# Gate products of a gated recurrence: eight matmuls a tile over stacked high and low parts, in place of twelve

## The chip, the cores and the metric

One core of a Trainium2 chip runs the program. The metric is device time in microseconds, and less is better. Before the change it was 1309.05 us, the median of three runs from 1308.57 to 1309.22.

## What is computed

A hybrid encoder of two layers takes one step for two groups of tokens that share the weights: 512 prompt tokens and 32 sample tokens, 544 columns in all. Each layer multiplies the stream by `w_in`, and the columns of the result feed three branches: attention in a band of chunks (A), retention (B) and a gated recurrence (C). The branches are gated and merged, and a projection, a per-layer embedding and a LayerNorm follow. The change is in branch C, of which the reference says:

```python
xpad = jnp.concatenate([s_conv.astype(xr.dtype), xr], axis=1)
xc = conv_b + sum(xpad[:, j:j + t] * conv_w[j] for j in range(CONV_W))
...
xb = xc.reshape(b, t, N_BLOCKS_C, BLOCK_C)          # 8 blocks of 64 channels
r = sigmoid(einsum('btni,nij->btnj', xb, w_gate_a) + b_gate_a)
ig = sigmoid(einsum('btni,nij->btnj', xb, w_gate_x) + b_gate_x)
log_a = -LRU_C * r * softplus(-lru_lambda)
a = jnp.exp(log_a)
bx = jnp.sqrt(-jnp.expm1(2.0 * log_a)) * ig * xc
h = scan of  h = a * h + bx
```

So each of eight blocks of 64 channels is multiplied by two 64 x 64 matrices, one for each gate.

## The kernel before

Activations lie transposed in SBUF: a tile has 128 channels on the partitions and the tokens along the free dimension. Every weight matrix is cut into blocks of 128 x 128, which come from HBM in chunks of eight (512 KB, `raw`). Every number that goes into a large product is split into a high part in a format that TensorE multiplies fast (fp32r) and a low part, the rest. `hilo` (lines 263 to 265) does that for activations: ScalarE casts the high part, VectorE subtracts it from the source. `split` (lines 208 to 213) does the same for weights, half a chunk at a time. A product is then three: high by high, high weight by low activation, low weight by high activation. One weight block over 544 tokens is therefore six matmuls (three products in two column spans), issued by `block` at line 256, and the text calls these six a block.

The order of the whole program is written out by a small planner in Python; the hardware queues then run it in that order, each engine for itself. `UNITS` lists the products of a layer: `xr` tiles 0 and 1 as a pair (16 blocks), `xr` 2, `xr` 3, then `va` 0 to 3, `qa` and `ka` in turn, and so on, 8 blocks each. Before each block the loop calls `tick` (line 174). A tick first lets `stream` (line 219) split weights up to eight blocks ahead, and then resumes those side jobs whose time has come:

```python
def add(job, delay=1):
    jobs.append([job, clock[0] + delay])
...
    stream(LEAD if clock[0] > 8 else 2)
    for j in list(jobs):
        while j[1] <= clock[0]:
            d = next(j[0], None)
```

Side jobs are generators; the numbers that they yield are steps of this clock, one step a block, and stand in the table `PACE`. When the second half of a chunk is split, `load` (line 195) issues the transfer of a later chunk into the buffer that was read last: this transfer waits in SP's queue for the subtraction that reads the buffer. All transfers of the program are issued by SP, in program order.

The recurrence is such a side job. When an `xr` tile is finished, `evac` copies it into `xrp` (lines 899 and 900) and adds `lru_tile(t)` (line 904). This computes the convolution `xc`, 547 columns (512 prompt tokens, three columns of padding and state, 32 sample tokens), with one instruction on ScalarE and three on VectorE; waits `lt1` = 8 steps; splits it with `hilo`; waits `lt2` = 5 steps; and then for each of the two gates issues six matmuls (line 522) with block-diagonal weights of 128 x 128 that hold two 64 x 64 matrices, over two halves of 274 columns in two PSUM banks, followed by three sigmoids on ScalarE (lines 525 to 527). The gates are `lt3` = 3 steps apart. At the end GpSimd multiplies the second gate by `xc` (lines 529 and 530). Four tiles make a layer; tile 1 begins 8 steps after the pair is done, and the others 2 steps after their product. After tile 3 the job `lru_job` does Exp, Tanh, Sqrt and the scan. In the same stretch the `va` tiles come out of TensorE, are copied from PSUM (line 866), and turned by TensorE later (`va_job`). Attention begins when the turned v, the gates and the first K are there (line 367).

PSUM has four kinds of buffers: `mm` (two of two banks each, for the large products), `sc` (two banks), `tp` (one) and `pv` (one). Small tiles in SBUF come from the pool `tmp` with 14 buffers.

Of the kernel before, what the change touches and what calls it, by code (L numbers as in the profile page):

```python
# [9 lines left out]
F32 = mybir.dt.float32  # L10
F32R = mybir.dt.float32r
AF = mybir.ActivationFunctionType
ALU = mybir.AluOpType
MUL, ADD, SUB = ALU.mult, ALU.add, ALU.subtract
# [3 lines left out]
NP, NS = 512, 32  # L18
N = NP + NS
# [36 lines left out]
def blocks_of(kind):  # L56
# [5 lines left out]
NB = len(BLOCKS)  # L62
NCH = NB // 8
AT = {k: BLOCKS.index((k, 0, 0)) for k in ("xr", "wg", "pg")}
# [5 lines left out]
PACE = {  # L70
# [5 lines left out]

# [10 lines left out]

P_CW, P_CB, P_BA, P_BX, P_LAM, P_GN, P_LG, P_LB = 0, 16, 20, 24, 28, 32, 36, 44
P_SC, P_SL = 52, 64
P_S0 = 68  # L90
NPAR = P_S0 + 256


# [30 lines left out]
def encoder(ctx: ExitStack, tc, xT, pT, W, RB, KC, VC, PAR, CST, LGB, o_y, o_k, o_v, o_rp, o_rs, o_cv, o_lr):  # L124
    nc = tc.nc
    V, S, G, T, Q = nc.vector, nc.scalar, nc.gpsimd, nc.tensor, nc.sync
# [6 lines left out]
    tp_ = pool("tmp", 14)  # L133
# [9 lines left out]
    def sl(name, dt=F32, shape=(128, 4, N)):  # L143
        return slab.tile(list(shape), dt, tag="slab", name=name)

    def tmp(name, shape=(128, N)):
        return tp_.tile(list(shape), F32, tag="tmp", name=name)

    def psum(kind):
        if kind == "mm":  # L150
            return ps_mm.tile([128, 1024], F32, tag="mm", name="mm")
        return {"sc": ps_sc, "tp": ps_tp, "pv": ps_pv}[kind].tile([128, 512], F32, tag=kind, name=kind)
# [18 lines left out]
    def add(job, delay=1):  # L171
        jobs.append([job, clock[0] + delay])
# [19 lines left out]
    raw, parts, held = {}, {}, {}  # L192
# [70 lines left out]
    def hilo(h, lo, src):  # L263
        S.copy(h, src)  # L264
        V.tensor_tensor(lo, src, h.bitcast(F32), SUB)  # L265
# [59 lines left out]
    def layer(l, env, nxt):  # L325
        pa = par[l]

        def pcol(c, t):
            return pa[:, c + t:c + t + 1]
# [172 lines left out]
        W547 = NP + 3 + NS  # L502

        def lru_tile(t):
            if t == 0:
                env["lru"] = [sl("lru_r"), sl("lru_i"), sl("lru_a")]
            R, I, _ = env["lru"]
            xrp = env["xrp"]
            xc = tmp("xc", (128, W547))
            S.activation(xc, xrp[:, t, 0:W547], AF.Identity, scale=pcol(P_CW, t), bias=pcol(P_CB, t))  # L510
            for j in range(1, 4):
                V.scalar_tensor_tensor(xc, xrp[:, t, j:j + W547], pcol(P_CW + 4 * j, t), xc, MUL, ADD)
            yield PACE["lt1"]
            xch, xcl = (tp_.tile([128, W547], F32R, tag="tmp", name="xch") for _ in range(2))
            hilo(xch, xcl, xc)
            yield PACE["lt2"]
            for g in range(2):
                w, lo = ([parts[(l * NB + AT["wg"] + g * 4 + t) // 4][i][:, t] for i in range(2)])
                ps = psum("sc"), psum("pv")
                for i, (wg, x) in enumerate(((w, xch), (w, xcl), (lo, xch))):  # L520
                    for p_, c0 in ((ps[0], 0), (ps[1], W547 - 274)):
                        T.matmul(p_[:, :274], lhsT=wg, rhs=x[:, c0:c0 + 274], start=i == 0, stop=i == 2)  # L522
                d = (I if g else R)[:, t]
                b_ = pcol(P_BX if g else P_BA, t)
                S.activation(d[:, :274], ps[0][:, :274], AF.Sigmoid, bias=b_)
                S.activation(d[:, 274:NP], ps[1][:, 1:NP - 273], AF.Sigmoid, bias=b_)
                S.activation(d[:, NP:], ps[1][:, 274 - NS:274], AF.Sigmoid, bias=b_)
                yield PACE["lt3"]
            G.tensor_tensor(I[:, t, :NP], I[:, t, :NP], xc[:, :NP], MUL)
            G.tensor_tensor(I[:, t, NP:], I[:, t, NP:], xc[:, NP + 3:], MUL)  # L530
            if t == 3:
                env["gates"] = True
                add(lru_job())

        def lru_job():
            R, I, A = env["lru"]

            for t in range(4):
                S.activation(A[:, t], R[:, t], AF.Exp, scale=sp[:, 1, l, t:t + 1])
                S.activation(R[:, t], R[:, t], AF.Tanh, scale=sp[:, 0, l, t:t + 1])  # L540
                yield PACE["lru0"]
            y = I
            for t in range(4):
                r, a = R[:, t], A[:, t]
                V.scalar_tensor_tensor(r, a, 1.0, r, ADD, MUL)
                V.tensor_scalar(a, r, -1.0, 1.0, MUL, ADD)
                V.scalar_tensor_tensor(r, a, 1.0, r, ADD, MUL)
                yield PACE["lru1"]
            for t in range(4):
                S.activation(R[:, t], R[:, t], AF.Sqrt)  # L550
                yield PACE["lru2"]
            for t in range(4):
                G.tensor_tensor(R[:, t], R[:, t], I[:, t], MUL)
                yield PACE["lru3"]
                V.tensor_tensor_scan(y[:, t, :NP], A[:, t, :NP], R[:, t, :NP], 0.0, MUL, ADD)
                V.tensor_tensor_scan(y[:, t, NP:], A[:, t, NP:], R[:, t, NP:], pcol(P_SL, t), MUL, ADD)
            yield 2
            env["yc"] = y
            Q.dma_start(out=o_lr[l, :, :, 0:1], in_=y[:, :, NP - 1:NP])
            Q.dma_start(out=o_lr[l, :, :, 1:2], in_=y[:, :, N - 1:N])  # L560
# [20 lines left out]
        def ret_job():  # L581
# [41 lines left out]
            g128 = bc(cst[:, C_G128:C_G128 + 4], [[1, 4], [0, 64]])  # L623
            s0 = e3(pa[:, P_S0:P_S0 + 256])
            for c in range(4):
# [230 lines left out]
        def evac(kind, t, ps, hf=None):  # L856
            pv = ps[:, MM0:MM0 + N]
            if kind in KEY:
# [3 lines left out]
                d = env[key][:, t]  # L862
                if kind == "kb":
                    S.mul(d, pv, 0.125)
                else:
                    S.copy(d, pv)
                if kind == "ka":
                    if t == 0:
                        env["KTh"], env["KTl"] = sl("KTh", F32R), sl("KTl", F32R)
# [23 lines left out]
            elif kind == "xr":  # L893
# [7 lines left out]
                if t == 3:  # L901
                    Q.dma_start(out=o_cv[l, :, :, 0:3], in_=xrp[:, :, NP:NP + 3])
                    Q.dma_start(out=o_cv[l, :, :, 3:6], in_=xrp[:, :, NP + NS + 3:NP + NS + 6])
                add(lru_tile(t), PACE["lt00"] if t == 1 else PACE["lt0"])
            elif kind in ("za", "zb", "zc"):
                for f in {"za": ("ya1", "ya2"), "zb": ("yb",), "zc": ("yc",)}[kind]:
                    need(env, f)
                y = env["y" + kind[1]]
                if t == 0:
                    env[kind] = (sl(kind + "h", F32R), sl(kind + "l", F32R))  # L910
                h, lo = env[kind]
# [12 lines left out]
            elif kind[0] == "b":  # L924
                sg = env.pop(("sg", t))
                a, b = t // 4, t % 4
# [19 lines left out]
            elif kind == "wo":  # L946
                a, b = t // 4, t % 4
                if b == 0:
                    env["r", a] = sl("r")
                r, xh_, xl_ = env["r", a][:, b], st["xh"][a][:, b], st["xl"][a][:, b]  # L950
# [48 lines left out]
        for group in UNITS:  # L999
            kind, t = group[0]  # L1000
# [27 lines left out]
            for k in range(nk):  # L1028
                for ps in pss:
                    a, b = k // 4, k % 4  # L1030
# [117 lines left out]
```

## Time and profile before

| | us |
|---|---|
| median of three runs | 1309.05 |
| the profiled execution's own time | 1308.99 |
| its span, from the first to the last instruction | 1307.2 |
| TensorE busy (matmul) | 1290.2 |
| VectorE busy | 719.6 |
| ScalarE busy | 547.0 |
| GpSimd busy | 176.3 |

The engines are written PE (TensorE), ACT (ScalarE), DVE (VectorE), POOL (GpSimd) and SP, which issues the transfers; SPq is its queue. In a row of the timeline the first number is the start in microseconds from the beginning of the span and the second the duration; then come the engine, the line of the kernel, the operation, the tile that is written and after the arrow those that are read, partitions by elements, and how many such instructions the row merges. What stands in brackets is the idle time before it and what ended that. In a row of transfers the last number is the median time from issue to landing.

### The profile page before, as it was taken

The page shows a single profiled execution, that of the slowest core. Times are in us where ns is not written, and L with a number is a line of the kernel's source. Part 1 is how long each engine was busy: PE and PEld are TensorE (multiplying, and loading weights), DVE is VectorE, ACT ScalarE, POOL GpSimd, SP SyncE. Part 2 cuts the span into 40 slices and gives each one's busy share as a digit, 9 for nine tenths or more (in the row PEclk, how much of TensorE's full clock was granted, in tenths as well). Part 3 has the DMA queues.
Part 4 walks back from the last instruction along what each step waited for, and adds up shares of the span by engine and source line. Part 5 has one row for each costly group of instructions (what it writes and reads, how often), then busy time and mean ns, then how long its engine had stood idle before and what let it go on. Part 6 is the DMA issues. An engine that isn't in the chain of part 4 may idle for free.

```text
span 1307.2 us, 25090 instructions
## 1 busy us (share of the span) xinstructions
PE 1290.2 (99%) x10552; PEld 1255.8 (96%) x10552; DVE 719.6 (55%) x1273; ACT 547.0 (42%) x1083; POOL 176.3 (13%) x158
## 2 busy tenths in 40 slices
PE   9999999999999999999999999999999999999996
PEld 9999889999999999999989998999999999999996
DVE  5666663563754443455584756626637534434567
ACT  6665544323632233323277655443235322332231
POOL 0210121410101101000032102125001011010000
PEclk9999999999999999999999999999999999999998
DMA  7333522321222222434132335222212222224231
GB/s 285 132 131 98 174 66 83 96 92 51 96 81 82 98 80 82 165 101 143 65 112 72 130 99 166 74 83 89 87 62 81 98 81 89 90 82 166 81 114 69
DMA packets 44609, 134.80 MB, mean 103 GB/s; under 512 B 9488, under 2 KB 11792, under 8 KB 42704
## 3 DMA queue, kind: packets, MB, share of 16 engines
q1 hardware_dynamic: 44496, 133.20, 30.6%
q8 instruction: 83, 1.36, 0.5%
q14 instruction: 30, 0.25, 0.1%
HBM read 117.02 MB, written 11.70 MB: 98 GB/s over the span
## 4 chain that ended last, share of the span: by engine, by line
PE 95%; DVE 3%; DMA 1%; ACT 1%; issue 0%; SPq 0%; POOL 0%; DVEq 0%
PE mm L256 84%; PE sc L407 2%; PE pv L441 1%; PE tp L423 1%; PE tp L334 1%; DMA raw<-in_W 1%; PE sc L667 1%; PE pv L690 1%; PE pv L522 0%; DVE r L819 0%; PE sc L522 0%; DVE xl L265 0%; PE sc L750 0%; PE sc L603 0%; PE pv L685 0%; PE sc L494 0%
## 5 line engine op out<-in xcount | busy, mean ns | idle before, releaser
L256 PE MATMUL mm<-xh,wh 128*128 128x288 f32 x2144 | 455.5, 294 | 0.4 <-ACT xrp L900 0.4
L256 PE MATMUL mm<-xh,wl 128*128 128x288 f32 x2144 | 444.2, 288 | 0.0
L256 PE MATMUL mm<-xl,wh 128*128 128x288 f32 x2144 | 442.8, 288 | 0.0
L212 DVE TENSOR_TENSOR wl<-raw,wh 128x512 fp32r<-128x512 f32 (+1 forms) x354 | 262.6, 760 | 282.3 <-ACT wh L211 277.2
L256 PEld LDWEIGHTS mm<-xh,wh 128*128 128x128 f32 x2144 | 328.4, 189 | 10.8 <-issue 7.5
L256 PEld LDWEIGHTS mm<-xl,wh 128*128 128x128 f32 x2144 | 328.8, 188 | 0.0
L256 PEld LDWEIGHTS mm<-xh,wl 128*128 128x128 f32 x2144 | 328.6, 188 | 0.0
L211 ACT CAST wh<-raw 128x512 fp32r<-128x512 f32 (+1 forms) x354 | 208.2, 614 | 36.0 <-PE mm L256 30.8
L922 ACT ACTIVATE sg<-mm 128x544 f32<-128x544 f32 x48 | 30.0, 625 | 154.0 <-PE mm L256 154.0
L934 POOL TENSOR_TENSOR m<-m,sg 128x544 f32<-128x544 f32 x30 | 46.8, 1561 | 316.7 <-DVE sg L932 316.7
L359 ACT ACTIVATE sx<-sx,sst 128x128 f32<-128x128 f32 (+4 forms) x68 | 38.0, 559 | 67.1 <-DVE sst L357 60.2
L256 PE MATMUL mm<-xh,held 128*128 128x288 f32 (+1 forms) x320 | 64.1, 292 | 0.3 <-ACT ple L942 0.3
L256 PE MATMUL mm<-mh,wh 128*128 128x288 f32 (+1 forms) x256 | 53.0, 288 | 0.0
L256 PE MATMUL mm<-mh,wl 128*128 128x288 f32 (+1 forms) x256 | 53.0, 288 | 0.0
L256 PE MATMUL mm<-ml,wh 128*128 128x288 f32 (+1 forms) x256 | 52.8, 287 | 0.0
L256 PEld LDWEIGHTS mm<-xh,held 128*128 128x128 f32 x320 | 51.3, 188 | 0.6 <-ACT ple L942 0.5
L256 PE MATMUL mm<-xl,held 128*128 128x288 f32 (+1 forms) x160 | 46.4, 290 | 0.6 <-DVE xl L265 0.6
L264 ACT CAST xh<-r 128x544 fp32r<-128x544 f32 (+2 forms) x32 | 17.0, 532 | 68.3 <-DVE r L952 64.1
L932 DVE TENSOR_TENSOR sg<-mm,sg 128x544 f32<-128x544 f32 x32 | 23.2, 725 | 37.0 <-PE mm L256 37.0
L913 ACT ACTIVATE z<-mm 128x544 f32<-128x544 f32 x24 | 15.0, 626 | 60.6 <-PE mm L256 60.5
L571 POOL TENSOR_TENSOR swap<-swap,cst 128x544 f32<-128x544 f32 x16 | 24.9, 1554 | 108.3 <-DMA swap<-QB 32.1
L256 PEld LDWEIGHTS mm<-mh,wh 128*128 128x128 f32 x256 | 39.4, 189 | 0.0
(251 smaller groups left out, 1783.4 us busy)
## 6 DMA issues: line engine op xcount, KB each, us to landing
raw<-in_W SPq DMA_DIRECT2D x189, 512.0 KB, 3.3
pled<-ple SPq DMA_DIRECT2D x4, 1088.0 KB, 9.8
ple<-pled SPq DMA_DIRECT2D x4, 1088.0 KB, 7.0
bias<-in_RB SPq DMA_DIRECT2D x16, 256.0 KB, 3.7
x<-in_xT SPq DMA_DIRECT2D x4, 544.0 KB, 9.5
o_v<-VA SPq DMA_DIRECT2D x2, 1088.0 KB, 4.6
o_k<-KT SPq DMA_DIRECT2D x2, 1088.0 KB, 5.1
swap<-KB SPq DMA_DIRECT2D x32, 68.0 KB, 2.0
```

The lines of the kernel that those rows point to most:

```text
L211: S.copy(h[:, k:k + step], t)
L212: V.tensor_tensor(lo[:, k:k + step], t, h[:, k:k + step].bitcast(F32), SUB)
L256: T.matmul(ps[:, MM0 + a:MM0 + b], lhsT=w[:, n % 4, :], rhs=x[:, a:b], start=first and i == 0, stop=last and i == 2)
L264: S.copy(h, src)
L334: T.transpose(tp[:rows, t * 128:(t + 1) * 128], src[:, t, c0:c0 + rows], ident)
L359: S.activation(x, x, AF.Exp, bias=s[:, 0:1], scale=-1.0, accum_out=s[:, 1:2])
L407: T.matmul(scs[j][:, o:o + n], lhsT=q_[r, p, i * 128:i * 128 + 128], rhs=k_[r, p, :n], start=k == 0, stop=k == 2)
L571: G.tensor_tensor(sw, sw, cst[:, C_SIN:C_SIN + N], MUL)
L913: S.activation(z, pv, AF.Sigmoid)
L922: S.activation(sg, pv, AF.Sigmoid)
L932: V.tensor_tensor(sg, pv, sg, MUL)
L934: (V if kind == "bB" and t == 7 else G).tensor_tensor(m, m, sg, ADD)
```

## The change

Each gate product works on 64-channel blocks in place of 128-channel tiles. For the block `b` of a tile a new tile `xs[b]` holds 128 partitions: the block's 64 high rows and its 64 low rows, stacked. The high rows keep their partitions, the low rows go to the other half. [...] The weights are laid out on the host so that both halves of the partitions hold the same 64 x 128 matrix, w_gate_a beside w_gate_x. One product with the high part of this matrix then gives high by high and high by low for both gates at once, and one with the low part adds low by high (and low by low). That is two products in two column halves for each of two blocks: eight matmuls a tile instead of twelve. Rows 0 to 63 and 64 to 127 of the result belong to different gates, so there are four sigmoids for each block, 64 partitions each; the biases of the second gate are stored a second time, rolled by 64 (`P_BXS`). The gate tiles keep all 547 columns, and GpSimd's multiply becomes one instruction.

The first block's products use the two `sc` banks, the second's `pv` and `tp`. The tiles begin at new times: `lt0` is a delay for each tile, (2, 11, 12, 13), so that counted from the end of the pair they begin at steps 2, 11, 20 and 29 (before: 2, 8, 10 and 18). Three paces of `lru_job` go from 3 to 2. The copies of the `va` tiles out of PSUM go from ScalarE to VectorE.

```diff
-    "sa3": 3, "lt0": 2, "lt00": 8, "lt1": 8, "lt2": 5, "lt3": 3, "lru0": 3, "lru1": 3, "lru2": 1, "lru3": 3,
+    "sa3": 3, "lt0": (2, 11, 12, 13), "lt1": 8, "lt2": 5, "lt3": 3, "lru0": 2, "lru1": 2, "lru2": 1, "lru3": 2,
...
-            xch, xcl = (tp_.tile([128, W547], F32R, tag="tmp", name="xch") for _ in range(2))
+            xch, xcl, *xs = (tp_.tile([128, W547], F32R, tag="tmp", name="xhl") for _ in range(4))
+            rows = slice(0, 64), slice(64, 128)
             hilo(xch, xcl, xc)
+            for b in range(2):
+                Q.dma_start(out=xs[b][rows[b]].bitcast(F32), in_=xch[rows[b]].bitcast(F32))
+                Q.dma_start(out=xs[b][rows[1 - b]].bitcast(F32), in_=xcl[rows[b]].bitcast(F32))
             yield PACE["lt2"]
-            for g in range(2):
-                w, lo = ([parts[(l * NB + AT["wg"] + g * 4 + t) // 4][i][:, t] for i in range(2)])
-                ps = psum("sc"), psum("pv")
-                for i, (wg, x) in enumerate(((w, xch), (w, xcl), (lo, xch))):
+            for b in range(2):
+                n = l * NB + AT["wg"] + 2 * t + b
+                ps = [psum(k) for k in (("pv", "tp") if b else ("sc", "sc"))]
+                for i in range(2):
                     for p_, c0 in ((ps[0], 0), (ps[1], W547 - 274)):
-                        T.matmul(p_[:, :274], lhsT=wg, rhs=x[:, c0:c0 + 274], start=i == 0, stop=i == 2)
-                d = (I if g else R)[:, t]
-                b_ = pcol(P_BX if g else P_BA, t)
-                S.activation(d[:, :274], ps[0][:, :274], AF.Sigmoid, bias=b_)
-                S.activation(d[:, 274:NP], ps[1][:, 1:NP - 273], AF.Sigmoid, bias=b_)
-                S.activation(d[:, NP:], ps[1][:, 274 - NS:274], AF.Sigmoid, bias=b_)
+                        T.matmul(p_[:, :274], lhsT=parts[n // 4][i][:, n % 4], rhs=xs[b][:, c0:c0 + 274],
+                                 start=i == 0, stop=i == 1)
+
+                for d, r, b_ in ((R, rows[b], P_BA), (I, rows[1 - b], P_BXS)):
+                    b_ = pcol(b_, t)[r]
+                    S.activation(d[rows[b], t, :274], ps[0][r, :274], AF.Sigmoid, bias=b_)
+                    S.activation(d[rows[b], t, 274:], ps[1][r, 1:274], AF.Sigmoid, bias=b_)
                 yield PACE["lt3"]
-            G.tensor_tensor(I[:, t, :NP], I[:, t, :NP], xc[:, :NP], MUL)
-            G.tensor_tensor(I[:, t, NP:], I[:, t, NP:], xc[:, NP + 3:], MUL)
+            G.tensor_tensor(I[:, t], I[:, t], xc, MUL)
...
-                    S.copy(d, pv)
+                    (V.tensor_copy if kind == "va" else S.copy)(d, pv)
...
-                add(lru_tile(t), PACE["lt00"] if t == 1 else PACE["lt0"])
+                add(lru_tile(t), PACE["lt0"][t])
...
-                W[l, n // 8, :, n % 8] = 0
-                for b in range(2):
-                    r = slice(64 * b, 64 * b + 64)
-                    W[l, n // 8, r, n % 8, r] = g["w_gate_x" if k // 4 else "w_gate_a"][l, 2 * (k % 4) + b]
+                ax = [g[a][l, k] for a in ("w_gate_a", "w_gate_x")]
+                W[l, n // 8, :, n % 8] = np.tile(np.concatenate(ax[::-1] if k % 2 else ax, 1), (2, 1))
```

Two places of the new order matter for what follows. The first is ScalarE in layer 0 around tile 1's high part. Before, the rows stand so: three sigmoids of tile 0's first gate, then the cast of tile 1 (`xch_628`), and later those of the second gate and the cast of tile 2 (`xch_664`).

```order
L525 ACTIVATE lru_r_482<-sc_611,par0_91 128x274
L526 ACTIVATE lru_r_482<-pv_612,par0_91 128x238
L527 ACTIVATE lru_r_482<-pv_612,par0_91 128x32
L264 CAST xch_628<-xc_538 128x547
L899 COPY xrp_462<-mm_551 128x512
L900 COPY xrp_462<-mm_551 128x32
L211 CAST wh_643<-raw_438 128x512
L525 ACTIVATE lru_i_483<-sc_653,par0_91 128x274
L526 ACTIVATE lru_i_483<-pv_654,par0_91 128x238
L527 ACTIVATE lru_i_483<-pv_654,par0_91 128x32
L264 CAST xch_664<-xc_568 128x547
```

After, on the same engine, the four sigmoids of tile 0's second group (banks `pv_649` and `tp_650`) stand ahead of the cast of tile 1 (`xhl_665`), and the convolution of tile 2 behind it.

```order
L533 ACTIVATE lru_r_482<-pv_649,par0_91 64x274
L534 ACTIVATE lru_r_482<-tp_650,par0_91 64x273
L533 ACTIVATE lru_i_483<-pv_649,par0_91 64x274
L534 ACTIVATE lru_i_483<-tp_650,par0_91 64x273
L265 CAST xhl_665<-xc_577 128x547
L511 ACTIVATE xc_681<-xrp_462,par0_91 128x547
```

The cast moved from behind the first group of the tile before to behind its second group; tiles 2 and 3 have it in the same way, and for tile 3 a cast of weights (`wh_870`) stands between the sigmoids and the cast.

The second place is SP's queue in layer 0 from the padding's output on. Before, only loads of weights follow (`raw`), then the output of v.

```order
L902 DMA o_cv<-xrp_462 512x1x3
L903 DMA o_cv<-xrp_462 512x1x3
L203 DMA raw_695<-in_W 128x1024
L203 DMA raw_808<-in_W 128x1024
L203 DMA raw_892<-in_W 128x1024
L203 DMA raw_960<-in_W 128x1024
L878 DMA o_v<-VA_756 128x2176
```

After, from tile 2's transfers on: `xhl_770` and `xhl_771` are its two stacked tiles, `xhl_878` and `xhl_879` those of tile 3.

```order
L520 DMA xhl_770<-xhl_768 64x547
L521 DMA xhl_770<-xhl_769 64x547
L520 DMA xhl_771<-xhl_768 64x547
L521 DMA xhl_771<-xhl_769 64x547
L204 DMA raw_788<-in_W 128x1024
L204 DMA raw_874<-in_W 128x1024
L520 DMA xhl_878<-xhl_876 64x547
L521 DMA xhl_878<-xhl_877 64x547
L520 DMA xhl_879<-xhl_876 64x547
L521 DMA xhl_879<-xhl_877 64x547
L204 DMA raw_955<-in_W 128x1024
```

Four transfers a tile came in between the loads; those of tile 2 stand ahead of the load of their stretch, those of tile 3 directly behind one (`raw_874`).

More of the change, by code (lines that the diff above doesn't have):

```diff
@@ L89 @@
 P_SC, P_SL = 52, 64
-P_S0 = 68
+P_BXS = 68
+P_S0 = 72
 NPAR = P_S0 + 256
@@ L505, in lru_tile @@
             if t == 0:
-                env["lru"] = [sl("lru_r"), sl("lru_i"), sl("lru_a")]
+                env["lru"] = [sl(k, shape=(128, 4, W547)) for k in ("lru_r", "lru_i", "lru_a")]
             R, I, _ = env["lru"]
@@ L541, in lru_job @@
                 yield PACE["lru0"]
-            y = I
+            y = I[:, :, :N]
             for t in range(4):
@@ L555, in lru_job @@
                 V.tensor_tensor_scan(y[:, t, :NP], A[:, t, :NP], R[:, t, :NP], 0.0, MUL, ADD)
-                V.tensor_tensor_scan(y[:, t, NP:], A[:, t, NP:], R[:, t, NP:], pcol(P_SL, t), MUL, ADD)
+                V.tensor_tensor_scan(y[:, t, NP:], A[:, t, NP + 3:], R[:, t, NP + 3:], pcol(P_SL, t), MUL, ADD)
             yield 2
@@ L1113 @@
             put(c, feat(g[k][l], t))
+        put(P_BXS, np.roll(feat(g["b_gate_x"][l], 4), 64, 0))
         put(P_SC, feat(g["state_conv"][l, 0], 4))
```

## The prediction

> **What bounds the kernel now.** First the page, for the shares, TensorE's clock and the chain that ended last, and under them the first row of PE's list of waits (total, times, longest).
>
> ```profile
> span 1307.2 us, 25090 instructions
> PE 1290.2 (99%) x10552; PEld 1255.8 (96%) x10552; DVE 719.6 (55%) x1273; ACT 547.0 (42%) x1083; POOL 176.3 (13%) x158
> PEclk9999999999999999999999999999999999999998
> PE 95%; DVE 3%; DMA 1%; ACT 1%; issue 0%; SPq 0%; POOL 0%; DVEq 0%
> PE tp L750 <- DVE r L968: 2.0, 2, 1.4
> ```
>
> TensorE is never without work, and 95% of the chain is its own. So a matmul taken out is worth its slot in full, and each time TensorE must wait counts in full too. Next, PE's rows in the timeline, from the last blocks of layer 0's recurrence: the last gate of a tile, then ordinary blocks (six matmuls, here three rows of two).
>
> ```profile
> 61.76 0.29 PE L522 MATMUL sc<-xch,held 128*128 128x274 f32 x1
> 62.39 0.29 PE L522 MATMUL pv<-xch,held 128*128 128x274 f32 x1
> 62.52 0.41 PE L256 MATMUL mm<-xh,wh 128*128 128x288 f32 x2
> 64.78 0.42 PE L256 MATMUL mm<-xh,wh 128*128 128x288 f32 x2
> ```
>
> The durations overlap; the starts give the price. Six gate matmuls take 62.52 - 61.76 = 0.76, or 0.127 us each. Three blocks take 64.78 - 62.52 = 2.26, or 0.753 us each: this is the length of one step of the program's clock.
>
> **What is taken away.** A tile issues 8 gate matmuls of 274 columns for 12. Eight tiles (four in each layer) save 32 x 0.127 = 4.1 us, all on the path. Line 522's own answer shows one more thing that goes:
>
> ```profile
>   ACT lru_r L527: 0.6, 2
> ```
>
> Twice a gate waited for a sigmoid to empty its bank, where two tiles ran into each other (0.6 us together). With tiles nine steps apart and four banks in turn, this goes. The gain is 4.7 us.
>
> **What is added on the path.** Each tile's matmuls now need data that went from ScalarE (the high part) to VectorE (the low part) to a transfer. PACE leaves the distance between hilo and the first group at 5 steps, 3.8 us. But for tiles 1 to 3 ScalarE cannot start at hilo's place: by the new order the four sigmoids of the tile before, which read its second group, stand ahead of the high part, and they wait for TensorE. I call S the start of that second group. TensorE then has 4 x 0.127 + 6 x 0.753 = 5.0 us of work until the next tile's first group. Is the data there by S + 5.0? Of ACT, PE, DVE and POOL around 45 to 48 us:
>
> ```profile
> 45.22 0.29 PE L522 MATMUL sc<-xch,held 128*128 128x274 f32 x1
> 45.55 0.49 ACT L525 ACTIVATE lru_i<-sc,par 128x274 f32<-128x274 f32 x1 [0.20 <-PE sc L522]
> 45.93 0.45 ACT L526 ACTIVATE lru_i<-pv,par 128x238 f32<-128x238 f32 x1
> 46.44 0.66 ACT L264 CAST xch<-xc 128x547 fp32r<-128x547 f32 x1
> 47.13 1.21 DVE L265 TENSOR_TENSOR xch<-xc,xch 128x547 fp32r<-128x547 f32 x1 [1.06 <-ACT xch L264]
> 46.46 1.30 POOL L529 TENSOR_TENSOR lru_i<-lru_i,xc 128x512 f32<-128x512 f32 x1 [46.02 <-ACT lru_i L526]
> 44.10 0.73 DVE L265 TENSOR_TENSOR xch<-xc,xch 128x547 fp32r<-128x547 f32 x1
> ```
>
> The sigmoid follows the bank's last matmul by 45.55 - 45.22 = 0.33. The first bank's last is the third matmul, at S + 0.25, so the first sigmoid starts at S + 0.58. A 274-column sigmoid occupies ScalarE for 45.93 - 45.55 = 0.38; that it has 64 partitions now saves nothing:
>
> ```profile
> 90.22 0.56 ACT L335 COPY vatoks<-tp 32x512 f32<-32x512 f32 x1
> 86.39 0.57 ACT L335 COPY vatok<-tp 128x512 f32<-128x512 f32 x1
> ```
>
> 32 partitions take as long as 128. Four sigmoids end at S + 2.1; VectorE starts 47.13 - 46.44 = 0.69 after the cast did, at S + 2.8. The same four sigmoids release GpSimd's multiply by xc, which starts with the cast (46.46). Beside it the subtraction took 1.21 instead of 0.73, and ended 0.58 after GpSimd did (48.34 against 47.76): VectorE seems to stand until GpSimd is done. The multiply is now one instruction of 547 columns, an estimated 1.37 from 1.30 for 512. So the low part is done at S + 2.1 + 1.37 + 0.58 = S + 4.05. If GpSimd does not hold it, S + 3.5.
>
> The nearest transfer is the swap of the rotary step, 32 partitions from SBUF to SBUF:
>
> ```profile
> 215.81 0.61 ACT L866 COPY QB<-mm 128x544 f32<-128x544 f32 x1 [0.93 <-PE mm L256]
> 216.45 0.51 SPq L567 DMA_DIRECT2D swap<-QB  x1
> 218.27 0.59 SPq L568 DMA_DIRECT2D swap<-QB  x1
> 220.39 0.72 DVE L570 TENSOR_TENSOR QB<-QB,cst 128x544 f32<-128x544 f32 x1 [0.38 <-DMA swap<-QB]
> DMA to landing us min/median/max: 1.9/2.0/3.7
> swap<-QB SPq DMA_DIRECT2D x32, 68.0 KB, 2.0
> o_y<-tk SPq DMA_DIRECT2D x6, 256.0 KB, 2.1
> ```
>
> SP issues 0.03 after the producer's end (216.42), each issue holds SP for some 0.6, and the reader starts 220.39 - 218.27 = 2.12 after the last issue. Ours move 64 partitions, 137 KB, between the 68 KB and the 256 KB of these rows; I add 0.1: 2.25 from the low part to TensorE. [...] The high part's transfer is issued earlier, and the second group's two, 0.6 and 1.2 later, have three blocks more: no wait of theirs.
>
> Tiles 1 and 2: data at S + 4.05 + 2.25 = 6.3 against 5.0, a wait of 1.3 each. From below 0.7 (S + 3.5 for the low part), from above 2.
>
> Tile 3: its hilo falls on a step in which half a chunk of weights is split and the next raw load is emitted. So a cast of wh stands ahead of the high part, its subtraction ahead of the low part, and the raw load (waiting for that subtraction) ahead of our four transfers in SP's queue. The weights' subtraction is then the one that stands behind GpSimd and ends at S + 4.05; raw is issued by S + 4.45, and ours behind it. What that costs shows in the one place where swaps followed a raw load at once, on SP and in the answer on transfers of 145 to 146.6 us:
>
> ```profile
> 144.21 1.04 SPq L203 DMA_DIRECT2D raw<-in_W  x1
> 145.34 0.62 SPq L567 DMA_DIRECT2D swap<-KB  x1
> 146.01 0.58 SPq L568 DMA_DIRECT2D swap<-KB  x1
> swap<-KB SPq DMA_DIRECT2D x2, 68.0 KB, 3.3
> ```
>
> The two landed on average 3.3 after issue, 3.7 after raw's issue ended at 145.25. With twice the bytes I take 4.0: S + 8.4, and 8.5 with the reader's start. The wait is 3.5; from below 1.5 (no hold by GpSimd, no queueing behind raw: two more operations of some 0.55 and an SP issue before ours).
>
> Tile 0 has no sigmoids ahead; its distance from hilo counts. Layer 0, then layer 1:
>
> ```profile
> 38.44 0.66 ACT L264 CAST xch<-xc 128x547 fp32r<-128x547 f32 x1
> 40.26 0.72 DVE L265 TENSOR_TENSOR xch<-xc,xch 128x547 fp32r<-128x547 f32 x1
> 41.68 0.29 PE L522 MATMUL sc<-xch,held 128*128 128x274 f32 x1
> 687.77 0.72 DVE L265 TENSOR_TENSOR xch<-xc,xch 128x547 fp32r<-128x547 f32 x1
> 690.26 0.29 PE L522 MATMUL sc<-xch,held 128*128 128x274 f32 x1
> ```
>
> In layer 1 the low part ends at 688.49; plus 2.25 is 690.74, 0.5 after the matmul's old start. In layer 0 the subtraction stood behind tile 1's convolution, which moves back by three steps; I put its end at 40.15 (cast, weights, two small steps of the rates), so 42.4 against 41.68: 0.7. If it stays at 40.98, 1.5.
>
> **Hidden, at nothing.** Two sigmoids more a tile, the v copies on VectorE in place of ScalarE, three columns more in the recurrence: these engines are busy 42% and 55%, and TensorE meets them only in the chains above. The gates come 11 steps later, but attention also waits for K and the turned v, later still; lru_job's shorter paces give the steps back. The turning of v now runs beside Exp and Tanh on ScalarE; if its copies lag, up to 0.5 a layer. Beside the stalls I take none.
>
> **The sum.** Waits: 0.7 + 0.5 + 4 x 1.3 + 2 x 3.5 = 13.4. Less 4.7: 8.7 us longer. The profiled execution took 1308.99 us, next to the median of 1309.05, so 1317.7 us. About 0.2%, 2.6 us, is what a measurement can tell from no change.
>
> **Rivals.** *No hold and no queue*: GpSimd's multiply delays nothing, and tile 3's transfers are not held by raw's. For it: 44.10 shows the short subtraction. Against: 47.13 and the 3.3 us. Waits 1.2 + 4 x 0.6 + 2 x 1.5 = 6.6, result 1308.99 + 6.6 - 4.7 = 1310.9: no change. Chance 0.15.
>
> *The transfers land in time* (faster): the chain of S + 6.3 would have to be under S + 5.0, for instance with a transfer of under 1 us. Then the matmuls' price alone remains: 1304.3. Against it stands the least of 1.9 us for any swap and that sigmoids cannot precede their matmuls. It also holds if part of the wait were already there before, which the page's list of PE's waits doesn't show. Chance 0.10.
>
> [...] Chance 0.12.
>
> **The numbers.** My forecast has 0.63, with its own range 1313 to 1321. Slower is forecast and clock, 0.75; same 0.15; faster 0.10. The range, 1308.5 to 1323, takes in the second rival from below and the clock from above, and leaves out the case of 1304 and doubled waits.
>
> **What would show it.** After: the gate matmuls 64, with starts 0.127 apart; PE's list of waits led by the gate line released by the xhl transfers, 8 times, none for the second groups; tile 3's the longest at over 3 us, with raw issued just ahead; the low part's subtraction at about 1.2 in tiles 1 and 2. If that list shows no wait on xhl the forecast is wrong outright; if all waits are under 1 us, the hold and the queue are.

## The result, and the profile after

The changed kernel takes 1347.31 us (median of five runs, 1345.52 to 1350.32) against 1308.74 for the one before: a ratio of 1.0301, with a 95% interval from 1.0285 to 1.0317. That is 38.6 us slower, where 8.7 were forecast. The direction was right, the size was not, and 1347 lies far outside the range that ended at 1323.

The page after, with the rows that answer to those of before:

```profile
span 1345.5 us, 25138 instructions
PE 1300.9 (97%) x10520; PEld 1262.8 (94%) x10520; DVE 729.3 (54%) x1281; ACT 555.9 (41%) x1091; POOL 174.1 (13%) x150
PEclk9988999999999999999999989999999999999998
PE 86%; DVE 7%; ACT 4%; DMA 2%; issue 1%; POOL 0%; DVEq 0%; ACTq 0%
```

TensorE lacks 32 matmuls, and yet it is busy 10.7 us longer; its idle time, span less busy, went from 17.0 to 44.6. The second number is waits. The first can only be slower matmuls, and the row of the clock shows an 8 in three slices where it had a 9. The list of TensorE's waits (us in total, times, longest):

```profile
PE sc L528 <- DMA xhl<-xhl: 18.2, 8, 4.3
PE tp L424 <- DVE sx L365: 8.6, 2, 4.8
PE tp L756 <- DVE r L974: 2.0, 2, 1.4
PE mm L257 <- DVE wl L213: 1.7, 2, 0.8
```

The first row is the forecast's: eight waits on the stacked tiles, here 18.2 us instead of 13.4. The second was not in it: attention's first transposes, once in each layer, wait for VectorE's normalized scores (lines 364 and 365). The third was there before; the fourth, 0.8 us in each layer, is new. Next, stretches of layer 0, and the last of layer 1. Behind the length of a stretch stand the busy times of TensorE's matmuls, its weight loads, VectorE, ScalarE and GpSimd (with the number of instructions), then the granted clock (1.00 is full), the share of the DMA engines and GB/s:

```profile
36.00:50.70 14.70, 13.88 (x111) 13.68 (x109) 8.08 (x18) 11.11 (x22) 1.37 (x1) 1.00 0.59 174
50.70:61.00 10.30, 7.38 (x47) 7.18 (x47) 4.01 (x6) 4.49 (x10) 0.38 (x1) 0.83 0.35 96
61.00:72.00 11.00, 9.63 (x77) 9.45 (x76) 6.60 (x9) 7.14 (x15) 1.93 (x2) 1.00 0.37 100
72.00:88.00 16.00, 11.87 (x75) 11.67 (x74) 3.61 (x6) 7.39 (x14) 1.36 (x1) 0.79 0.35 114
115.00:131.00 16.00, 11.16 (x66) 9.89 (x66) 11.32 (x33) 7.34 (x22) 2.60 (x3) 0.79 0.32 58
781.00:800.00 19.00, 15.21 (x94) 13.36 (x93) 12.80 (x35) 9.27 (x26) 1.48 (x3) 0.82 0.44 84
```

A mean of 0.83 over 10.3 us is 3.5 us at half speed, 0.79 over 16 is 6.7. The trace's record of the clock has five such stretches ahead of the kernel's end, of 3.41 or 6.83 us at a granted 0.50, 27.3 in all. Before had none there. TensorE idles for 2.3 us of them, and half of the rest, 12.5, is lost to the slow clock. So 27.6 of idle time and 12.5 of slow clock, less 4.1 for the matmuls, make 36.0 of the 38.3 us by which the span grew; 2.3 us have no name.

**The waits on the stacked tiles**, tile by tile: in layer 0 0.82, 2.92, 1.37 and 4.13, in layer 1 0.55, 2.66, 1.41 and 4.35. The forecast had 0.7 (0.5 in layer 1), 1.3, 1.3 and 3.5. Tile 1 in layer 0, on all engines:

```profile
45.92 0.64 SPq L908 DMA_DIRECT2D o_cv<-xrp  x1
46.65 0.59 SPq L909 DMA_DIRECT2D o_cv<-xrp  x1
...
47.92 0.47 ACT L534 ACTIVATE lru_i<-tp,par 64x273 f32<-64x273 f32 x1
48.41 0.65 ACT L265 CAST xhl<-xc 128x547 fp32r<-128x547 f32 x1
48.46 1.37 POOL L536 TENSOR_TENSOR lru_i<-lru_i,xc 128x547 f32<-128x547 f32 x1 [48.02 <-ACT lru_i L534]
...
49.09 1.33 DVE L266 TENSOR_TENSOR xhl<-xc,xhl 128x547 fp32r<-128x547 f32 x1 [1.74 <-ACT xhl L265]
...
50.45 1.48 SPq L521 DMA_DIRECT2D xhl<-xhl  x1
...
53.87 0.75 PE L528 MATMUL sc<-xhl,held 128*128 128x274 f32 x4 [2.92 <-DMA xhl<-xhl]
```

The cast stands behind the last sigmoid, GpSimd starts its 1.37 with it, the subtraction takes 1.33 and ends 0.59 after GpSimd: all as forecast. Then the transfer of the low part is issued at 50.45, and the matmuls come 3.45 after the low part (50.42), where 2.25 had been taken and tile 2 shows 2.43. Ahead of it went the two transfers of the padding. Of the transfers issued from 44 to 52 us (the last number is the median to landing):

```profile
xhl<-xhl SPq DMA_DIRECT2D x3, 136.8 KB, 3.3
o_cv<-xrp SPq DMA_DIRECT2D x2, 6.0 KB, 4.9
```

Those of 6 KB, 512 rows of 12 bytes, take longer than anything around them. Tile 3:

```profile
71.75 0.33 SPq L204 DMA_DIRECT2D raw<-in_W  x1
72.19 0.47 SPq L520 DMA_DIRECT2D xhl<-xhl  x1
...
72.75 0.55 SPq L521 DMA_DIRECT2D xhl<-xhl  x1
...
76.97 1.25 PE L528 MATMUL sc<-xhl,held 128*128 128x274 f32 x4 [4.13 <-DMA xhl<-xhl]
```

Raw stands just ahead, and the matmuls start 4.9 us after the end of its issue (72.08); 4.1 had been taken.

**Attention's start**, layer 0: GpSimd, VectorE and TensorE.

```profile
104.27 5.24 POOL L559 TENSOR_TENSOR lru_r<-lru_r,lru_i 128x547 f32<-128x547 f32 x3 [18.25 <-ACT lru_r L556]
...
106.55 3.51 DVE L213 TENSOR_TENSOR wl<-raw,wh 128x512 fp32r<-128x512 f32 x2
...
108.80 0.33 PE L408 MATMUL sc<-KTh,QTh 64*128 64x128 f32 x2
...
109.98 1.21 DVE L561 TENSOR_TENSOR_SCAN lru_i<-lru_a,lru_r 128x512 f32<-128x512 f32 x1
...
113.36 1.22 DVE L561 TENSOR_TENSOR_SCAN lru_i<-lru_a,lru_r 128x512 f32<-128x512 f32 x1
...
115.50 0.29 DVE L358 CUSTOM_DVE_ANT_0 sx<-sc,bias 128x128 f32<-128x128 f32 x1 [0.75 <-POOL bias L380]
...
116.06 1.22 DVE L561 TENSOR_TENSOR_SCAN lru_i<-lru_a,lru_r 128x512 f32<-128x512 f32 x1
...
117.20 1.30 DVE L562 TENSOR_TENSOR_SCAN lru_i<-lru_a,par,lru_r 128x32 f32<-128x32 f32 x1
...
119.01 1.21 DVE L561 TENSOR_TENSOR_SCAN lru_i<-lru_a,lru_r 128x512 f32<-128x512 f32 x1
...
120.48 0.29 DVE L365 TENSOR_SCALAR sx<-sx,sst 128x128 f32<-128x128 f32 x1
...
120.82 1.15 PE L424 MATMUL tp<-cst,sx 128*128 128x128 f32 x3 [4.84 <-DVE sx L365]
```

This is the end of `lru_job`. The same step before:

```profile
95.03 0.33 PE L407 MATMUL sc<-KTh,QTh 64*128 64x128 f32 x2
...
97.14 0.28 DVE L357 CUSTOM_DVE_ANT_0 sx<-sc,bias 128x128 f32<-128x128 f32 x1
...
97.70 1.22 DVE L555 TENSOR_TENSOR_SCAN lru_i<-lru_a,lru_r 128x512 f32<-128x512 f32 x1
...
101.32 0.29 DVE L364 TENSOR_SCALAR sx<-sx,sst 128x128 f32<-128x128 f32 x1
```

TensorE issues the scores at 108.80 (before 95.03), VectorE begins on them 6.7 us later (before 2.1), and normalizes the first another 5.0 us later (before 4.2). So most of the delay lies ahead of VectorE's first score: beside three multiplies on GpSimd two weights' subtractions took 3.51 instead of 2 x 0.69, and two of the four pairs of scans stand behind these. All four pairs now fall between TensorE's scores and their normalization. Before only one did, and TensorE did not wait.

### The profile page after: what moved, and what is told of

The parts are those of the page before. It is cut to its first block, busy times and chain, and to the rows that moved or that the text cites. A ratio compares the mean times of both kernels' runs of the same rounds, so it can differ in the third digit from the quotient of the medians.

```text
span 1345.5 us, 25138 instructions
## 1 busy us (share of the span) xinstructions
PE 1300.9 (97%) x10520; PEld 1262.8 (94%) x10520; DVE 729.3 (54%) x1281; ACT 555.9 (41%) x1091; POOL 174.1 (13%) x150
## 4 chain that ended last, share of the span: by engine, by line
PE 86%; DVE 7%; ACT 4%; DMA 2%; issue 1%; POOL 0%; DVEq 0%; ACTq 0%
PE mm L257 76%; DMA xhl<-xhl 2%; PE sc L408 1%; PE tp L424 1%; PE pv L442 1%; DVE wl L213 1%; PE tp L335 1%; PE sc L673 1%; PE pv L696 1%; ACT wh L212 1%; DVE lru_i L561 1%; DVE xhl L266 1%; DMA raw<-in_W 0%; PE sc L528 0%; DVE r L825 0%
## 5 line engine op out<-in xcount | busy, mean ns | idle before, releaser
L213 DVE TENSOR_TENSOR wl<-raw,wh 128x512 fp32r<-128x512 f32 (+1 forms) x354 | 265.5, 767 | 283.2 <-ACT wh L212 278.4
```

The source lines that it names most:

```text
L213: V.tensor_tensor(lo[:, k:k + step], t, h[:, k:k + step].bitcast(F32), SUB)
```

## The experiments

Theory 1: there are two lots of waits, on the stacked tiles and at attention's start, the second from the new times of the recurrence alone, and the half clock follows from both. Its rivals put the loss on the new products, on the copies of v, on the bias of attention, or on one queue. All edits are to the changed kernel where nothing else is said; the kernel before ran on the same chip each time and took 1307.9 to 1309.0 (medians).

**Without the transfers.** The products read the high and the low part as they are, so the gates are others.

```diff
-            for b in range(2):
-                Q.dma_start(out=xs[b][rows[b]].bitcast(F32), in_=xch[rows[b]].bitcast(F32))
-                Q.dma_start(out=xs[b][rows[1 - b]].bitcast(F32), in_=xcl[rows[b]].bitcast(F32))
+            xs = xch, xcl
```

> The changed kernel without its four transfers a tile: the products read the high and the low tile directly, so the gates' values are not those of the reference; everything else, and every instruction's place, stays. Theory 1 (three costs add up: 18.2 us of waits for the transfers, 8.6 us of waits of attention's first transposes for VectorE because the recurrence's tail now falls into attention's start, and 13.7 us because TensorE's clock was halved for 27.3 us after the long waits; less 4.7): the waits on the gate matmuls go, the 8.6 us and the half clock behind them stay, so 1317 to 1323 us. Theory 2 (attention's wait is only the echo of the late, stalled recurrence): all goes, 1304 us.

1321.4 us, ratio 1.0095 (1.0066 to 1.0124). The first two rows of the list of TensorE's waits:

```profile
PE tp L424 <- DVE sx L365: 9.1, 2, 5.1
PE tp L754 <- DVE r L972: 2.0, 2, 1.4
```

No wait on the stacked tiles, those of attention are left, and two stretches of 6.83 us at half clock, both there (the granted clock is 0.83 from 95 to 115 us, 0.992 over the run). So the transfers cost 26 us with their clock, and a loss of 12 remains that has nothing to do with them, the saved matmuls already deducted.

**The kernel before, with the new times alone.** Twelve products, no transfers, copies of v by ScalarE:

```diff
-    "sa3": 3, "lt0": 2, "lt00": 8, "lt1": 8, "lt2": 5, "lt3": 3, "lru0": 3, "lru1": 3, "lru2": 1, "lru3": 3,
+    "sa3": 3, "lt0": (2, 11, 12, 13), "lt1": 8, "lt2": 5, "lt3": 3, "lru0": 2, "lru1": 2, "lru2": 1, "lru3": 2,
...
-                add(lru_tile(t), PACE["lt00"] if t == 1 else PACE["lt0"])
+                add(lru_tile(t), PACE["lt0"][t])
```

> The kernel before with only the new start steps of the tiles (2, 11, 20, 29) and the new paces of the recurrence's tail: no transfers, twelve products, copies of v by ScalarE. Theory 1: no wait on the gates, but attention's first transposes wait some 4 us in each layer and the clock is halved behind that: 1308.7 + 8.6 + about 6.8 = 1324 us, or 1317 if the waits stay under the length that halves the clock. Theory 2 (the loss in attention comes from the transfers or from the copies of v on VectorE): 1308 to 1309 us.

1329.19 us, ratio 1.0155 (1.0125 to 1.0184):

```profile
PE tp L423 <- DVE sx L364: 8.5, 2, 4.5
PE tp L334 <- ACT vatok L335: 4.4, 2, 2.2
```

The new times alone cost 20 us, with no new product in the kernel: attention's wait, 17.1 us of half clock (0.991 over the run), and one that I had not expected, the turning of v behind ScalarE's copies (4.4 us, and 3.41 of the half clock behind it). These last, some 6 us, are not part of the changed kernel's loss.

**The copies of v back on ScalarE.**

```diff
-                    (V.tensor_copy if kind == "va" else S.copy)(d, pv)
+                    S.copy(d, pv)
```

> The changed kernel with the copies of v back on ScalarE. Theory 1: the copies carry neither loss; the same waits on the transfers (16 to 20 us) and in attention (6 to 10), 1343 to 1352 us. Rival (VectorE's four added copies a layer hold up the low part and push attention's work back): below 1335 us.

1351.04 us, 1.0322 (1.0292 to 1.0352). The turning of v waits 4.4 us (0.6 in the changed kernel), with a stretch of 3.41 at half clock behind each of its two waits. So that part of the change avoids 3.8 us of waits and is no cause of the loss. The time itself shows less: the two runs, 1350.31 and 1351.78, stand too near the changed kernel's highest, 1350.32, to tell the 3.7 us between the medians from scatter.

**The high and low parts earlier.** The same steps for the matmuls, but three more for the way there:

```diff
-    "sa3": 3, "lt0": (2, 11, 12, 13), "lt1": 8, "lt2": 5, "lt3": 3, "lru0": 2, "lru1": 2, "lru2": 1, "lru3": 2,
+    "sa3": 3, "lt0": (2, 11, 12, 13), "lt1": 5, "lt2": 8, "lt3": 3, "lru0": 2, "lru1": 2, "lru2": 1, "lru3": 2,
```

> The changed kernel with hilo and the transfers three steps earlier (lt1 5, lt2 8), the groups at the same steps. The casts now stand ahead of the sigmoids of the tile before and away from the load of weights. Theory 1: the waits on the transfers go (at most 1 us left), the clock is not halved there, attention's waits and the clock behind them stay: 1317 to 1323 us. Rival (transfers wait for their queue whenever they are issued): waits stay above 8 us, over 1330 us.

1328.02 us, 1.0146 (1.0116 to 1.0175), above the 1317 to 1323 of theory 1. The waits on the stacked tiles fall from 18.2 to 6.9, in three places instead of eight. What remains is in the queue: tile 0 of layer 0 stands behind a raw load (2.5), tile 2 behind the padding and raw (2.3 and 2.1). Attention's 8.4 stay. So more steps between cast and matmuls cure most, and not under 1 us, as I had thought.

**Six steps apart, and earlier parts.** Starts at steps 1, 7, 13 and 19, `lru_job` at its old paces:

```diff
-    "sa3": 3, "lt0": (2, 11, 12, 13), "lt1": 8, "lt2": 5, "lt3": 3, "lru0": 2, "lru1": 2, "lru2": 1, "lru3": 2,
+    "sa3": 3, "lt0": (1, 7, 5, 3), "lt1": 5, "lt2": 8, "lt3": 3, "lru0": 3, "lru1": 3, "lru2": 1, "lru3": 3,
```

> The changed kernel with hilo early (lt1 5, lt2 8), tiles six steps apart (they begin at steps 1, 7, 13 and 19 after the pair) and the old paces 3, 3, 1, 3 of the recurrence's tail, so the gates are done at step 38 where before had 37. Theory 1: no wait on transfers, no wait of attention, no half clock; what is left is the price of the matmuls, 1308.7 - 4.7 = 1304 us, at most 1306. Rival (four transfers a tile or eight 64-partition sigmoids cost TensorE something even with room): 1307 us or more.

1310.54 us, 1.0014 (1.0003 to 1.0025): 36.8 of the 38.6 us are gone with numbers of the table alone, and attention's wait is 0.8. The 1304 to 1306 were missed. Its rows of SP and TensorE show the one long wait:

```profile
36.14 0.33 SPq L204 DMA_DIRECT2D raw<-in_W  x1
36.52 0.57 SPq L520 DMA_DIRECT2D xhl<-xhl  x1
37.14 0.58 SPq L521 DMA_DIRECT2D xhl<-xhl  x1
...
43.69 1.25 PE L528 MATMUL sc<-xhl,held 128*128 128x274 f32 x4 [3.00 <-DMA xhl<-xhl]
```

The low part, issued at 37.14 behind raw, was there 6.5 us later. In this stretch the transfer engines are still busy with the first weights: their share from 36 to 44 us is 0.97. A half clock of 3.41 us followed: up to 47.0 us a pair of matmuls of a block takes 0.45 us, where it takes 0.25 behind that.

**The padding's output later.** The changed kernel, with the two transfers of 12-byte rows moved behind the end of `lru_job`:

```diff
-                if t == 3:
-                    Q.dma_start(out=o_cv[l, :, :, 0:3], in_=xrp[:, :, NP:NP + 3])
-                    Q.dma_start(out=o_cv[l, :, :, 3:6], in_=xrp[:, :, NP + NS + 3:NP + NS + 6])
...
             Q.dma_start(out=o_lr[l, :, :, 0:1], in_=y[:, :, NP - 1:NP])
+            xrp = env["xrp"]
+            Q.dma_start(out=o_cv[l, :, :, 0:3], in_=xrp[:, :, NP:NP + 3])
+            Q.dma_start(out=o_cv[l, :, :, 3:6], in_=xrp[:, :, NP + NS + 3:NP + NS + 6])
```

> The changed kernel with the two transfers of the padding (o_cv, 512 rows of 12 bytes each) moved behind the recurrence's tail. They were issued 1.3 and 2.0 us ahead of tile 1's first transfer, which took 3.3 to 4.0 us to land in place of 2.3. Theory 1: tile 1's waits fall from 2.9 and 2.7 to about 1.4 as tile 2's, and the half clock at 55 us (1.7 us lost) goes: 1340 to 1345 us. Rival (the queue of weights or SP's issue is what holds tile 1's transfers): waits of tile 1 stay above 2.5 us, time within 2 us of 1347.

1344.42 us, 1.0273 (1.0253 to 1.0294). TensorE's first matmuls of tile 1:

```profile
52.45 0.75 PE L528 MATMUL sc<-xhl,held 128*128 128x274 f32 x4 [1.91 <-DMA xhl<-xhl]
```

1.91 and, in layer 1, 1.92, where it was 2.92 and 2.66, and no half clock at 55 us any more. From the low part to the matmuls it is now 2.42 instead of 3.45, as in tile 2. So the padding cost tile 1 0.7 to 1.0 of its excess (by the rows it was issued 3.2 and 2.4 us ahead of the tile's first transfer, not 2.0 and 1.3); 0.5 over tile 2 remains, of which GpSimd's multiply (1.37 against 1.15) explains 0.2.

**A queue of their own.** The six-step kernel, its transfers issued by GpSimd:

```diff
-                Q.dma_start(out=xs[b][rows[b]].bitcast(F32), in_=xch[rows[b]].bitcast(F32))
-                Q.dma_start(out=xs[b][rows[1 - b]].bitcast(F32), in_=xcl[rows[b]].bitcast(F32))
+                G.dma_start(out=xs[b][rows[b]].bitcast(F32), in_=xch[rows[b]].bitcast(F32))
+                G.dma_start(out=xs[b][rows[1 - b]].bitcast(F32), in_=xcl[rows[b]].bitcast(F32))
```

> The six-apart kernel with the four transfers of a tile issued by GpSimd in place of SP, so they stand in another queue than the weights, the padding and the spills. Theory 1 (they land late because they stand behind raw and other transfers in SP's queue: in six-apart the first tile's landed 0.4 to 1.1 after a raw load that took 6.4 us): the 3.0 us wait of layer 0's first tile and the half clock behind it go, 1304 to 1307 us. Rival (the 16 engines are full at that time, whichever queue issues): the wait stays at 2 us or more, 1309 us or more.

1312.79 us, 1.004 (1.0025 to 1.0055). 4.0 us of waits on the stacked tiles, the longest 2.7, at the same place. So it isn't the order in SP's queue that holds them there. What is left are the transfer engines themselves, busy with weights in this run too (a share of 0.96 from 36 to 44 us); that they are the cause is argued, not shown.

**Clear of the raw load.** Starts moved to 4, 10, 15 and 21:

```diff
-    "sa3": 3, "lt0": (1, 7, 5, 3), "lt1": 5, "lt2": 8, "lt3": 3, "lru0": 3, "lru1": 3, "lru2": 1, "lru3": 3,
+    "sa3": 3, "lt0": (4, 10, 7, 5), "lt1": 5, "lt2": 8, "lt3": 3, "lru0": 2, "lru1": 3, "lru2": 1, "lru3": 3,
```

> The six-apart kernel with starts at steps 4, 10, 15 and 21, so that hilo falls on steps 9, 15, 20 and 26 and on none with a raw load or just behind one (5, 13, 21, 29), and pace 2 for Exp and Tanh. Theory 1: no wait on a transfer above 0.5 us, no half clock, attention's wait at most 1.5 us: 1304 to 1306 us. Rival (with gates done at step 40 in place of 38 the tail already reaches attention's start): attention's waits of 3 us or more, 1310 us or more.

1311.85 us (1309.17 to 1317.06), 1.0042 (1.0027 to 1.0056), where 1304 to 1306 was expected. The long wait is gone; tile 2 waits behind the padding (1.3 and 1.7), attention 1.4. No half clock in the profiled run of 1309.17; the others scatter, the three from 1314.7 to 1317.1 at a mean clock of 0.993 to 0.995, the rest at 0.996 or 0.997.

**The bias of attention earlier.** Its loads before the job's own waits:

```diff
         def attn_job():
+            bias_loads(0)
             while not all(k in env for k in ("vatok", "gates", ("K", 0))):
...
-            bias_loads(0)
```

> The changed kernel with attention's first two bias loads issued some steps earlier, before the job waits for its inputs, ahead of the raw load that held them in SP's queue. Their late landing let VectorE's first score instruction start 0.75 us late and ended 18 us of waiting by GpSimd. Theory 1a (in the tail's collision the late bias is what counts): the 8.6 us of waits before attention's transposes fall under 3 and the half clock behind them goes, 1333 to 1338 us. Theory 1b (VectorE's queue of scans and weights between the scores and their norm counts): they stay above 5 us, 1342 to 1348 us.

1350.43 us, 1.0326 (1.0305 to 1.0346). Attention waits 8.3 us as in the changed kernel, though VectorE's first score no longer waits for the bias. The releaser in front of that score (115.50) pointed at the bias; it was not the cause of TensorE's wait.

**Attention later.** The changed kernel, attention ten steps behind:

```diff
             bias_loads(0)
-            yield 4
+            yield 14
```

> The changed kernel with attention's first step 10 steps (7.5 us) later, behind the scans of the recurrence on VectorE; starts, transfers and all else as in the changed kernel. Theory 1 (the 8.6 us of waits of attention's first transposes come from sharing VectorE with the recurrence's end, and the half clock behind them from these waits): the waits on line 424 fall under 3 us, the two stretches of 6.83 at about 120 and 786 us go, and the time falls by 15 to 20 to 1327 to 1333; the 18 us of waits on the stacked tiles stay. Rival (attention starts late at whatever step, since its first operations wait for something else, such as the first K or the bias): the waits stay at 6 to 9 us and the time at 1343 to 1350.

1348.43 us, 1.0302 (1.0288 to 1.0316). The list of waits, and the two stretches that had stood at 0.79 and 0.82:

```profile
PE sc L528 <- DMA xhl<-xhl: 19.2, 8, 4.5
PE tp L482 <- ACT PT L430: 4.5, 2, 2.4
PE tp L482 <- ACT PT L485: 3.2, 2, 1.6
...
PE tp L424 <- DVE sst L364: 1.3, 2, 0.6
```

```profile
115.00:131.00 16.00, 15.30 (x120) 14.08 (x121) 11.37 (x32) 8.35 (x23) 0.14 (x1) 1.00 0.35 86
...
781.00:800.00 19.00, 18.29 (x143) 16.68 (x144) 12.86 (x37) 10.02 (x27) 0.14 (x1) 1.00 0.41 65
```

At its place the theory holds: 8.6 us of waits become 1.3, and the clock stays at 1.00. The time doesn't fall, against the theory's 1327 to 1333. The rest of attention moved too: the transposes of the sample group (line 482) now meet those of the prompt group in the one `tp` bank and wait 7.7 us for ScalarE's copies, and TensorE's idle time is 46.4 us instead of 44.6. With 10 us less of half clock (0.991 over the run instead of 0.987) some 3 us should still have been gained. They went into TensorE's busy time: counted at full clock it is 1291.7 us instead of 1288.4. Why its matmuls took longer stays open.

**Clear of both.** The kernel that clears the raw load, and the padding's output late as above; against the changed kernel:

```diff
-    "sa3": 3, "lt0": (2, 11, 12, 13), "lt1": 8, "lt2": 5, "lt3": 3, "lru0": 2, "lru1": 2, "lru2": 1, "lru3": 2,
+    "sa3": 3, "lt0": (4, 10, 7, 5), "lt1": 5, "lt2": 8, "lt3": 3, "lru0": 2, "lru1": 3, "lru2": 1, "lru3": 3,
...
-                if t == 3:
-                    Q.dma_start(out=o_cv[l, :, :, 0:3], in_=xrp[:, :, NP:NP + 3])
-                    Q.dma_start(out=o_cv[l, :, :, 3:6], in_=xrp[:, :, NP + NS + 3:NP + NS + 6])
```

> The nine-to-ten steps of the run that clears the raw load (starts 4, 10, 15, 21; high part 5 steps after the convolution, products 8 steps after that), and now the padding's output also behind the end of the recurrence. That run still had 3.0 us of waits on the stacked tiles, all in tile 2 behind the padding's output, and 1.4 us of waits of attention's first transposes. Theory (what is left there is the queue behind the padding's output, 12-byte rows): the waits on the stacked tiles fall under 1 us, and the time to 1304 to 1308, so a little faster than before (1308.7), since the saved matmuls are worth 4.1. Rival (they are late anyway, because the engines ahead of them are): 2 to 3 us of waits stay, 1308 to 1312.

1308.79 us, 1.0001 (0.9992 to 1.001).

```profile
PE tp L424 <- DVE sx L365: 2.6, 2, 2.0
...
PE sc L528 <- DMA xhl<-xhl: 0.5, 1, 0.5
```

The waits on the stacked tiles are gone, as expected (0.5), and it is 38.5 us faster than the change as it was made; yet it is no faster than before.

**Clear of the raw load, without transfers.** The first experiment's edit at these starts, the padding's output at its old place; the gates are again others:

```diff
-    "sa3": 3, "lt0": (2, 11, 12, 13), "lt1": 8, "lt2": 5, "lt3": 3, "lru0": 2, "lru1": 2, "lru2": 1, "lru3": 2,
+    "sa3": 3, "lt0": (4, 10, 7, 5), "lt1": 5, "lt2": 8, "lt3": 3, "lru0": 2, "lru1": 3, "lru2": 1, "lru3": 3,
...
-            for b in range(2):
-                Q.dma_start(out=xs[b][rows[b]].bitcast(F32), in_=xch[rows[b]].bitcast(F32))
-                Q.dma_start(out=xs[b][rows[1 - b]].bitcast(F32), in_=xcl[rows[b]].bitcast(F32))
+            xs = xch, xcl
```

> The run that clears the raw load, without the four transfers a tile: the products read the high part and the low part as they are, so the gates are not the reference's. This is the floor of the change at these starts. Theory (matmuls saved, and apart from waits on the transfers and attention's first transposes nothing is added): the 3.0 us of waits go, 1.4 at attention stay, 1304 to 1307, faster than before by 2 to 4. Rival (the change adds something else, on ScalarE or VectorE, that the list of waits doesn't name): 1308 or more.

1307.95 us, 0.9994 (0.9985 to 1.0003), where 1304 to 1307 was expected. So even transfers that cost nothing leave less than 0.2% at these starts. In the profiled run with transfers TensorE is busy 1287.6 (2.6 less than before, not 4.1) and idle 18.9 (1.9 more, attention's wait): 0.7 us shorter in the span. Attention's wait of 1.8 us was followed by 3.41 us at half clock in the run without transfers, and in the other, with 1.96, it was not (0.995 and 0.998 over the run). The gates do save what was forecast: from start to start their matmuls, with the waits among them, took 13.0 us before and take 8.4 with transfers, 4.6 less. But TensorE idles 2.0 us more elsewhere, and its other matmuls take 1.8 us more, 1.0 of it in the ordinary blocks and 0.6 in transposes; why these do is open.

## Why the prediction was wrong

*What went wrong first* is the paragraph "Hidden, at nothing": that the gates may come 11 steps later, since "attention also waits for K and the turned v, later still; lru_job's shorter paces give the steps back". That looks at when attention may begin, not at what stands on VectorE when it does. All four pairs of scans of `lru_job` fell into attention's first scores: 8.6 us of waits, and 13.66 us at half clock behind them. The kernel before with the new times alone shows it (8.5 us of waits), the run without transfers shows that the transfers have no part in it, and with attention later it is gone at its place. By the table the paces do give the steps back: the last pair of scans comes 76 steps after the `xr` pair, before 77. But the first comes at 70 instead of 68, and they are two steps apart instead of three. With the old paces and the last pair at step 78 (the six-step kernel) attention waited 0.8 us, so it isn't a late end as such that counts; but no run changes the paces alone. This term, taken as nothing, is 8.6 and up to half of 13.66, some 15 us.

*The clock* had a chance of 0.12 and the upper end of the range. No run shows the term that was taken for it; the changed kernel shows 27.3 us at a granted 0.50, in five stretches that cost 12.5. Three of the five are 6.83 us long, one of them behind tile 3, and tile 1 and attention have stretches too.

*The waits on the stacked tiles*: the mechanism was right, 13.4 should have been 18.2. Tile 2 and tile 0 were met to 0.1 (1.37 and 1.41 for 1.3; 0.82 and 0.55 for 0.7 and 0.5). Tile 1 was mis-sized by 1.6 and 1.4: the padding's transfers stood in the quoted order ahead of it, and I priced them at nothing; without them it is 1.9. Tile 3 was 4.13 and 4.35 for 3.5: raw was issued when forecast, and the matmuls came 4.9 after it instead of 4.1.

*Right*: eight waits, none for a second group; sigmoids ahead of the cast; the subtraction longer beside GpSimd's multiply (1.33, where it takes 0.72 alone); raw ahead of tile 3; 0.127 us for a matmul, and 4.6 us saved at the gates (in the run clear of both) for 4.7. The copies of v by VectorE avoid 3.8 us of waits.

*The rivals that ended at no change* needed transfers in time and an attention that doesn't care. Starts six steps apart bring both nearly about (1310.5).

## What to carry to other kernels

A step that is moved or packed closer must be followed to its end: what matters is not only who waits for its result but which queue its last operations stand in when the next stage begins. Where one engine is busy 99%, price a wait as its length plus the half clock that may follow: in the changed kernel each of TensorE's five waits of 2.9 us or more brought a stretch of 3.41 or 6.83 us, and those of 2.7 or less brought none, so that several small waits were cheaper there than one long (at other starts one of 1.8 brought one too). A transfer put between two engines needs slack for the queue that it meets, and the loads and small-row transfers issued just ahead of it belong into its price (here 4.9 us from the load's issue to tile 3's matmuls, and 1 us more for tile 1 behind the 12-byte rows).

## What the runs showed of the hardware

**The half clock came on a grid.** In the changed kernel's trace all stretches of half clock ahead of the end begin a whole number of 3.413 us apart, to within 0.1 (at 55.2, 75.6, 120.0, 744.7 and 785.6). Cut by that grid, its periods at full clock (the first 7.4 us, for which there is no record of the clock, and the last 20 left out; idle time by the matmul ends that the profile models) are of two kinds: in five TensorE was idle 2.1 us or more, and each was followed by a period at half clock; in the other 373 it was idle 1.8 or less, and none was. So what a wait cost depended on how it fell on the grid: tile 1's of 2.66 in layer 1 lies in two periods with 1.4 and 1.3 us idle and brought no half clock; tile 1's of 2.92 in layer 0 has 2.1 of it in one period and did. Of the eight periods at half clock three had idle time (0.2, 0.8 and 1.3) and were followed by another, and the five without any were not. Why it is so is not shown.

**VectorE beside GpSimd.** Two weights' subtractions took 3.51 us beside GpSimd's multiplies (0.69 each elsewhere), a 32-column scan 1.30 (0.26), and the subtraction of tile 1 took 1.33 and ended 0.59 us after GpSimd's multiply, where alone it takes 0.72. GpSimd's three multiplies took 5.24 (before 4.00).

**The transfers of small rows.** 6 KB in rows of 12 bytes took 4.9 us to land (the stacked tiles' 137 KB a median of 2.4), and the 137 KB behind them reached TensorE 1 us later than without them (3.45 against 2.42 from the low part).

**The formats.** In the kernel before, two matmuls with operands in fp32r (line 256, 544 columns together) take 0.25 us from start to start, a matmul with operands in f32 (line 685, 128 columns) 0.11: 0.46 and 0.87 ns a column.
